# A hybrid decoder layer on one core: down products fetched two chunks at a time, one of them in 8 banks, seven products summed further in PSUM, tables fetched ahead

## The chip, the cores and the metric

The kernel runs on one core of a Trainium2 chip. The metric is device time in microseconds of one execution; the median of three runs of the kernel before is 2338.41 us (2338.2 to 2345.58). All arithmetic is on float32 data. TensorE multiplies in the type float32r; to keep the precision each operand is split into a rounded part ("hi") and the rest ("lo"), and a product is summed from three matmuls: hi by hi, hi by lo, lo by hi.

## The reference

One layer of a decoder for 1024 prompt tokens and 8 x 4 sample tokens: a half-step SwiGLU, a mixer (a state-space scan beside windowed attention), a cross-attention into 256 memory tokens, and a second half-step SwiGLU, each between two RMS norms. The change lies in the two SwiGLUs (and in the preparation of the scan's tables, which runs beside the first one). D_MODEL is 1024, D_FF 2816.

```python
def rms_norm(x, g):
    xf = x.astype(jnp.float32)
    y = xf * lax.rsqrt(jnp.mean(xf * xf, axis=-1, keepdims=True) + RMS_EPS)
    return (y * g.astype(jnp.float32)).astype(x.dtype)

def swiglu(x, w_gate, w_up, w_down):
    return (jax.nn.silu(x @ w_gate) * (x @ w_up)) @ w_down

def decoder_layer(x, ...):
    h = x
    h = h + 0.5 * rms_norm(swiglu(rms_norm(h, p['ffn1_pre_g']), ...), p['ffn1_post_g'])
    z = rms_norm(h, p['mix_pre_g']) @ p['w_in']
    ...
    h = h + rms_norm(mixed, p['mix_post_g'])
    c = memory_attend(rms_norm(h, p['xa_pre_g']), mem_k, mem_v, p['w_mem_q'], p['w_mem_o'])
    h = h + rms_norm(c, p['xa_post_g'])
    h = h + 0.5 * rms_norm(swiglu(rms_norm(h, p['ffn2_pre_g']), ...), p['ffn2_post_g'])
    return h, ...
```

## The kernel before

The 1056 tokens are three thirds ("t") of NT = 352, kept with the channels on the 128 partitions; `ORDER = (2, 0, 1)` gives ta = 2 (the one with the sample tokens), tb = 0, tc = 1. The hidden width 2816 is NH = 22 chunks of 128. A matmul has 128 weights columns and 352 tokens, and goes to one PSUM bank.

Order of the work in a SwiGLU:

1. Gate and up of the third ta: `gate_up` for each of the 22 chunks (48 matmuls each, line 106), the product goes to HBM scratch `h1[j][:, 2]`, one scratch tensor a chunk.
2. The down product of ta: `down` with parts `((0, 8),)`, that is, one pass in which all 8 banks (6 of the tag `mm`, 2 of the tag `px`) hold the 8 output blocks. In each chunk k it loads the hidden chunk (`raw2`, 352 wide; 2 buffers), splits it into `hid` (line 247 ACT for hi, 248 DVE for lo; `hid` holds two chunks and has 2 buffers), loads and splits the weights' chunk (`loadw`: `raw`, 2 buffers; line 100 ACT, 101 DVE into `w`, 6 buffers of 1024 columns), and runs 3 matmuls for each bank (line 252).
3. Gate and up of the thirds tb and tc together, the "pair stage": `pair_gate_up`. A 2 x 2 block product (two row blocks of 512 channels, two thirds) is done with seven products instead of eight (Strassen-Winograd). `pair_operands` makes the seven sums of the tokens once; `pair_weights` makes the seven sums of the weights for every two chunks (lines 307 ACT, 308 DVE, 312 to 318 DVE); `pair_products` runs the seven products (84 matmuls, line 327) and combines them into c11, c12, c21, c22 with copies (line 334 ACT) and adds out of PSUM (336, 342, 344, 346, 348 DVE). There are 22 such sets in a SwiGLU, 11 of the gate and 11 of the up weights.
4. The down products of tb and tc. In the first SwiGLU both go in two passes of 4 banks, `((0, 4), (4, 4))`, and each pass reads the whole hidden tensor anew; in the second SwiGLU the first of them goes in one pass of 8.

After each down product follow the post-norm with the residual (`post1` or `finish2`: squares on ACT, their sum on DVE line 117, a few small matmuls of lines 152 and 144 for the statistic, lines 220 and 221 on DVE) and, in the first SwiGLU, the next norm's halves (`pre1`). The statistics use the two `px` banks.

Beside the first SwiGLU the scan's tables are prepared: `ssm_prep` is a generator of 42 pieces (phase1, small_tables, 8 of `tables`, 32 of `groups`; two pieces of `groups` make a pair with two transposes, line 691, and four small matmuls, line 697, in the `px` banks). `step()` runs the next piece; the stages call it as a "filler" between their own pieces: 9 times in gate/up, not in the first down product, once at each of the 22 fillers of the pair stage, and once a chunk in the last down products until none is left. `tables(q)` loads its start values `t0` from scratch right before it uses them.

What sets the order: a scheduler takes the instructions of the whole program with the program's order as priority, simulates them, and writes one fixed order for each engine; engines then wait for each other through semaphores. An engine runs its instructions strictly in that order. Loads go through SyncE's queue (SP), stores through ACT's.

Of the kernel before, what the change touches and what calls it, by code (L numbers as in the profile page):

```python
# [14 lines left out]
NT = 352  # L15
# [13 lines left out]
def decoder_step(tc, a, o):  # L29
# [208 lines left out]
    def down(wd, h, y, parts, rs=None, filler=lambda: None):  # L238
        for c0, n in parts:
            p = [bank() if c < 6 else pbank() for c in range(n)]  # L240
            for k in range(NH):
                if k % 2 == 0:
                    pair = hidden(2)
                x = R("raw2", [128, 1024], 2)[:, :NT]
                hi, lo = pair[:, k % 2, 0], pair[:, k % 2, 1]
                sy.dma_start(x, h[k])
                sc.activation(hi, x, AF.Copy)  # L247
                v.tensor_sub(lo, x, hi.bitcast(F32))  # L248
                w = loadw(wd[k][:, c0 * 128:(c0 + n) * 128], width=n * 128)
                for c in range(n):  # L250
                    for q, (wa, xa) in enumerate(PASSES):
                        pe.matmul(p[c][:, :NT], w[:, wa, c * 128:c * 128 + 128], (hi, lo)[xa],  # L252
                                  start=k == 0 and q == 0, stop=k == NH - 1 and q == 2)
                filler()
            for c in range(n):
                if rs is not None:
                    v.tensor_mul(y[:, c0 + c], p[c][:, :NT], rs)  # L257
                elif c % 2:
                    v.tensor_copy(y[:, c0 + c], p[c][:, :NT])
                else:  # L260
                    sc.activation(y[:, c0 + c], p[c][:, :NT], AF.Copy)
# [33 lines left out]
    def pair_weights(src, j, raws):  # L295
# [4 lines left out]
        free, ops = [], {}  # L300
# [9 lines left out]
        halves_of("a11", a11)  # L310
        halves_of("a22", a22)
# [11 lines left out]
    def pair_products(w, x, first, c12, c21, c22):  # L323
        def product(p, a_, b_, start=False, stop=True):
            for k in range(4):
                for i, (wa, xa) in enumerate(PASSES):
                    pe.matmul(p, w[a_][:, wa, k * 128:k * 128 + 128], x[b_][xa][:, k],  # L327
                              start=start and k == 0 and i == 0, stop=stop and k == 3 and i == 2,
                              skip_group_check=True)
# [4 lines left out]
        sc.activation(u, pa, AF.Copy)
        product(pb, "s2", "t2", True, True)
        v.tensor_add(u, u, pb)
# [5 lines left out]
        v.tensor_add(z, u, pc)  # L342
        product(pd, "s1", "t1", start=True)
        v.tensor_add(c22, z, pd)
        product(pc, "a22", "t4", stop=True)
        v.tensor_add(c21, u, pc)
        product(pd, "s4", "b22", stop=True)
        v.tensor_add(c12, u, pd)

    def pair_gate_up(x, wg, wu, hs, home, filler=lambda: None):  # L350
        gs = K8(home).rearrange("p (i k) n -> p i k n", i=2)

# [5 lines left out]
        for j in range(NH // 2):  # L358
            g = gs[:, j % 2]
            h = hidden(2).bitcast(F32).rearrange("p a b n -> p (a b) n")  # L360
            pair_products(pair_weights(wg, j, raws(0)), x, lambda p: sc.activation(g[:, 0], p, AF.Silu),
                          g[:, 1], g[:, 2], g[:, 3])
            sc.activation(g[:, 1:4], g[:, 1:4], AF.Silu)
            filler()
            pair_products(pair_weights(wu, j, raws(1)), x, lambda p: v.tensor_mul(h[:, 0], g[:, 0], p),
                          h[:, 1], h[:, 2], h[:, 3])
            v.tensor_mul(h[:, 1:4], h[:, 1:4], g[:, 1:4])
            for i in range(2):
                sc.dma_start(hs[2 * j + i], h[:, 2 * i:2 * i + 2])
            filler()  # L370
# [94 lines left out]
    def ssm_prep():  # L465
# [28 lines left out]
        cre, cim = take(32), take(32)  # L494
        base = pos[0]
# [126 lines left out]
        def small_tables():  # L622
# [7 lines left out]
            for q in range(8):  # L630
                sc.dma_start(t16[q], T[:, :, 4 * q:4 * q + 4])

        def tables(q):
# [4 lines left out]
            sc.activation(T[:, :, :, 0:16], t0, AF.Copy)  # L638
# [751 lines left out]
    pair_gate_up(ops, a["wg2"], a["wu2"], [h[:, 0:2] for h in h2], 2)  # L1390
# [130 lines left out]
```

## Time and profile before

| | |
|---|---|
| median of 3 runs | 2338.41 us |
| the profiled execution | 2338.15 us, its span 2336.4 us |
| mean granted clock of TensorE | 0.987 |
| PE busy | 2241.9 us, 96% of the span |
| DVE busy | 1667.1 us, 71% |
| ACT busy | 991.9 us, 42% |
| moved by DMA | 359.26 MB, mean 154 GB/s |

Stages by their matmuls (us from the span's start): gate/up of ta to 183, its down product to 269, pair stage 273 to 582, down products of tb and tc 582 to 822, mixer and cross-attention to about 1563, second gate/up of its first third to 1750, its down product to 1836, second pair stage to 2130, the last two down products to 2318, and the last norm to 2336.

How to read it: engines are PE (TensorE's matmuls), PEld (its weight loads), DVE (VectorE), ACT (ScalarE), POOL and SP. The profiler's matmul records overlap, since matmuls are pipelined: their mean is about twice the step between their starts. So a stage is judged by the number of matmuls in it. A name such as `w<-raw` is the written and the read tile; L100 is line 100; "DMA raw<-wd" is a load into the tile raw from the tensor wd.

### The profile page before, as it was taken

How to read it: one execution, taken by the hardware profiler on the slowest of the kernel's cores; microseconds unless marked ns; L12 is line 12 of the kernel's file. 1: busy time of each engine (PE TensorE's matmuls, PEld its weight loads, DVE VectorE, ACT ScalarE, POOL GpSimd, SP SyncE). 2: the span in 40 equal slices, each digit the busy share in tenths (PEclk: the TensorE clock that was granted, in tenths of full speed). 3: DMA queues.
4: the chain of work that ended last, by engine and by line, in shares of the span. 5: the costliest groups of instructions: out<-in, count | busy, mean ns of one | idle time of the engine just before them, and what ended most of it. 6: DMA issues, size and time to landing. Idle time of an engine off the chain costs nothing.

```text
span 2336.4 us, 37554 instructions
## 1 busy us (share of the span) xinstructions
PE 2241.9 (96%) x14141; PEld 2133.5 (91%) x14141; DVE 1667.1 (71%) x3621; ACT 991.9 (42%) x1872; POOL 8.6 (0%) x22
## 2 busy tenths in 40 slices
PE   8999999999788999999899989999999999999997
PEld 8999999999777899788699869999999999999987
DVE  7987899778657566777768855488746787775465
ACT  6434334434445522435644323344335433433353
POOL 0000000000000000000000000000000000000000
PEclk9999999999999999999899999999999999999998
DMA  7566545333676621544135562256656343326564
GB/s 257 177 185 206 170 152 163 114 118 120 202 212 196 206 91 55 183 143 131 49 97 158 168 231 80 64 164 200 221 165 203 109 150 110 103 97 191 166 201 144
DMA packets 167477, 359.26 MB, mean 154 GB/s; under 512 B 20064, under 2 KB 90208, under 8 KB 165856
## 3 DMA queue, kind: packets, MB, share of 16 engines
q1 hardware_dynamic: 118720, 298.28, 40.8%
q10 hardware_dynamic: 48576, 58.59, 7.2%
q8 instruction: 111, 1.82, 0.3%
q14 instruction: 70, 0.57, 0.1%
HBM read 300.32 MB, written 59.59 MB: 154 GB/s over the span
## 4 chain that ended last, share of the span: by engine, by line
PE 53%; DMA 11%; DVE 6%; ACT 3%; issue 1%; ACTq 0%; SPq 0%; DVEq 0%
PE mm L106 17%; PE mm L327 13%; PE mm L252 6%; DMA raw<-wd 5%; PE px L106 3%; DVE w L101 2%; PE px L252 2%; DMA raw<-h 2%; ACT w L100 1%; PE cs L1253 1%; PE cv L1278 1%; PE ac L876 1%; PE px L457 1%; PE px L1175 1%; DVE K L220 1%
## 5 line engine op out<-in xcount | busy, mean ns | idle before, releaser
L106 PE MATMUL mm<-X,w 128*128 128x352 f32 x4272 | 709.3, 326 | 10.8 <-ACT X L196 7.1
L106 PEld LDWEIGHTS mm<-X,w 128*128 128x128 f32 x4272 | 685.8, 188 | 25.5 <-ACT X L196 7.3
L252 PE MATMUL mm<-hid,w 128*128 128x352 f32 x2772 | 486.7, 331 | 39.9 <-ACT hid L247 25.7
L101 DVE TENSOR_TENSOR w<-raw,w 128x1024 fp32r<-128x1024 f32 (+1 forms) x359 | 368.5, 1028 | 198.4 <-ACT w L100 197.2
L252 PEld LDWEIGHTS mm<-hid,w 128*128 128x128 f32 x2772 | 456.0, 191 | 58.4 <-ACT hid L247 36.9
L100 ACT ACTIVATE w<-raw 128x1024 fp32r<-128x1024 f32 (+1 forms) x359 | 322.4, 900 | 412.4 <-DMA raw<-wd 129.3
L327 PE MATMUL mm<-xq,w 128*128 128x352 f32 x2112 | 359.8, 324 | 4.0 <-DVE K L257 4.0
L327 PEld LDWEIGHTS mm<-xq,w 128*128 128x128 f32 x2112 | 342.4, 189 | 6.0 <-DVE K L257 4.3
L307 ACT ACTIVATE w<-raw 128x512 fp32r<-128x512 f32 x308 | 178.4, 624 | 206.2 <-PE mm L327 119.8
L308 DVE TENSOR_TENSOR w<-raw,w 128x512 fp32r<-128x512 f32 x308 | 202.2, 687 | 15.8 <-ACT w L307 11.8
L327 PE MATMUL mm<-X,w 128*128 128x352 f32 x1056 | 185.7, 324 | 1.2 <-DVE sq L342 0.7
L327 PEld LDWEIGHTS mm<-X,w 128*128 128x128 f32 x1056 | 171.0, 188 | 3.3 <-DVE sq L342 1.0
L248 DVE TENSOR_TENSOR hid<-raw,hid 128x352 fp32r<-128x352 f32 x198 | 97.9, 521 | 64.5 <-ACT hid L247 60.1
L247 ACT ACTIVATE hid<-raw 128x352 fp32r<-128x352 f32 x198 | 90.6, 490 | 98.4 <-DMA raw<-h 50.9
L476 DVE TENSOR_TENSOR K<-K 128x256 f32<-128x256 f32 (+4 forms) x380 | 106.9, 320 | 26.2 <-DMA sp<-K 9.2
L117 DVE TENSOR_TENSOR tot<-tot,sq 128x352 f32<-128x352 f32 x179 | 93.1, 521 | 9.7 <-ACT sq L115 6.5
L327 PE MATMUL mm<-K,w 128*128 128x352 f32 x528 | 99.7, 326 | 0.0
L115 ACT ACTIVATE sq<-K 128x352 f32<-128x352 f32 x170 | 81.1, 488 | 35.7 <-DVE tot L117 26.1
L327 PEld LDWEIGHTS mm<-K,w 128*128 128x128 f32 x528 | 88.3, 190 | 0.3 <-ACT w L307 0.3
L252 PE MATMUL px<-hid,w 128*128 128x352 f32 x396 | 75.4, 324 | 0.0
L252 PEld LDWEIGHTS px<-hid,w 128*128 128x128 f32 x396 | 66.2, 188 | 0.0
L1210 ACT ACTIVATE K<-mm 128x352 f32<-128x352 f32 x48 | 22.3, 464 | 89.4 <-PE mm L106 89.2
(328 smaller groups left out, 2186.9 us busy)
## 6 DMA issues: line engine op xcount, KB each, us to landing
raw<-wu SPq DMA_DIRECT2D x87, 512.0 KB
raw<-wg SPq DMA_DIRECT2D x86, 512.0 KB
raw<-h SPq DMA_DIRECT2D x198, 176.0 KB
raw<-wd SPq DMA_DIRECT2D x66, 512.0 KB
raw<-wd SPq DMA_DIRECT2D x132, 256.0 KB
h<-hid ACTq DMA_DIRECT2D x44, 352.0 KB
sp<-sp SPq DMA_DIRECT2D x16, 848.0 KB
h<-K ACTq DMA_DIRECT2D x9, 1408.0 KB
```

The source lines that it names most:

```text
L100: sc.activation(w[:, 0], raw, AF.Copy)
L101: v.tensor_sub(w[:, 1], raw, w[:, 0].bitcast(F32))
L106: pe.matmul(p, w[:, wa, col:col + 128], x[xa][:, k, :n], start=first and i == 0, stop=last and i == 2)
L115: sc.activation(q, c, AF.Square)
L117: eng.tensor_add(tot, tot, q)
L247: sc.activation(hi, x, AF.Copy)
L248: v.tensor_sub(lo, x, hi.bitcast(F32))
L252: pe.matmul(p[c][:, :NT], w[:, wa, c * 128:c * 128 + 128], (hi, lo)[xa], start=k == 0 and q == 0, stop=k == NH - 1 and q == 2)
L307: sc.activation(w[:, 0], x, AF.Copy)
L308: v.tensor_sub(w[:, 1], x, w[:, 0].bitcast(F32))
L327: pe.matmul(p, w[a_][:, wa, k * 128:k * 128 + 128], x[b_][xa][:, k], start=start and k == 0 and i == 0, stop=stop and k == 3 and i == 2, s ...
L476: v.tensor_tensor(out, x, y, op)
```

## The change

Four things are changed.

- `down` takes the chunks two at a time: one load and one split for two hidden chunks (the scratch is now one tensor of 22 chunks for each third), and in a pass of 4 banks two loads of 512 columns into the two halves of one `raw` buffer with one split of 1024 columns. In a pass of 8 banks the weights are loaded as before. The down product of tb in the first SwiGLU goes in one pass of 8 banks instead of two of 4.
- `pair_products` sums further in PSUM: the bank pa takes P1, then s2t2, s3t3 and a22t4 on top, read in between (p1, u, z) or at the end; pd takes s1t1 and s4b22. Two adds on DVE are left out; two ACT copies come in. The last two products of a set run after the first product of the next set, and the sets share half-used weight tiles (`free`).
- The preparation's steps lie elsewhere: 4 in gate/up, 7 in the first down product (in chunks 0, 2, ..., 12), then two at each filler of the pair stage, but for the 12th, which holds `post1` of ta and the sum of squares of its next norm; `pre1_late` is left with the halves.
- `t0` is loaded one table ahead, into space of the tables that is free by then.

```diff
     def down(wd, h, y, parts, rs=None, filler=lambda: None):
         for c0, n in parts:
             p = [bank() if c < 6 else pbank() for c in range(n)]
-            for k in range(NH):
-                if k % 2 == 0:
-                    pair = hidden(2)
-                x = R("raw2", [128, 1024], 2)[:, :NT]
-                hi, lo = pair[:, k % 2, 0], pair[:, k % 2, 1]
-                sy.dma_start(x, h[k])
-                sc.activation(hi, x, AF.Copy)
-                v.tensor_sub(lo, x, hi.bitcast(F32))
-                w = loadw(wd[k][:, c0 * 128:(c0 + n) * 128], width=n * 128)
-                for c in range(n):
-                    for q, (wa, xa) in enumerate(PASSES):
-                        pe.matmul(p[c][:, :NT], w[:, wa, c * 128:c * 128 + 128], (hi, lo)[xa],
-                                  start=k == 0 and q == 0, stop=k == NH - 1 and q == 2)
-                filler()
+            for k in range(0, NH, 2):
+                x = R("raw2", [128, 1024], 2)[:, :2 * NT].rearrange("p (k n) -> p k n", k=2)
+                hid = hidden(2)
+                sy.dma_start(x, h[:, k:k + 2])
+                split(x, hid[:, :, 0], hid[:, :, 1])
+                if n == 8:
+                    ws = [loadw(wd[k + j]) for j in range(2)]
+                else:
+                    raw = wp.tile([128, 1024], F32, name="raw", tag="raw", bufs=2)
+                    for j in range(2):
+                        sy.dma_start(raw[:, 512 * j:512 * j + 512], wd[k + j][:, c0 * 128:c0 * 128 + 512])
+                    w = loadw(None, raw)
+                    ws = [w[:, :, 0:512], w[:, :, 512:1024]]
+                for j in range(2):
+                    for c in range(n):
+                        for q, (wa, xa) in enumerate(PASSES):
+                            pe.matmul(p[c][:, :NT], ws[j][:, wa, c * 128:c * 128 + 128], hid[:, j, xa],
+                                      start=k + j == 0 and q == 0, stop=k + j == NH - 1 and q == 2)
+                    filler()
...
-    def pair_products(w, x, first, c12, c21, c22):
+    def pair_products(w, x, out, c21):
...
-        pa, pb = bank()[:, :NT], bank()[:, :NT]
-        u = Q()
-        product(pa, "a11", "b11", start=True)
+        pa, pb, pd = (bank()[:, :NT] for _ in range(3))
+        p1, u, z = R("sg", [128, NT], 2), Q(), Q()
+        product(pa, "a11", "b11", True)
+        sc.activation(p1, pa, AF.Copy)
+        yield
+        product(pb, "a12", "b21", True)
+        v.tensor_add(out[:, 0], p1, pb)
+        product(pa, "s2", "t2", False)
         sc.activation(u, pa, AF.Copy)
-        product(pb, "s2", "t2", True, True)
-        v.tensor_add(u, u, pb)
-        product(pa, "a12", "b21", stop=True)
-        first(pa)
-        pc, pd = bank()[:, :NT], bank()[:, :NT]
-        z = S()
-        product(pc, "s3", "t3", start=True)
-        v.tensor_add(z, u, pc)
-        product(pd, "s1", "t1", start=True)
-        v.tensor_add(c22, z, pd)
-        product(pc, "a22", "t4", stop=True)
-        v.tensor_add(c21, u, pc)
-        product(pd, "s4", "b22", stop=True)
-        v.tensor_add(c12, u, pd)
+        product(pd, "s1", "t1", True)
+        product(pa, "s3", "t3", False)
+        sc.activation(z, pa, AF.Copy)
+        v.tensor_add(out[:, 2], z, pd)
+        yield
+        product(pa, "a22", "t4", False)
+        c21(pa)
+        product(pd, "s4", "b22", False)
+        v.tensor_add(out[:, 1], u, pd)
+        yield
...
+        def finish(n, steps, h):
+            next(steps)
+            j, g = n // 2, gs[:, n // 2 % 2]
+            if n % 2 == 0:
+                sc.activation(g[:, 0:3], g[:, 0:3], AF.Silu)
+            else:
+                v.tensor_mul(h[:, 0:3], h[:, 0:3], g[:, 0:3])
+                for i in range(2):
+                    sc.dma_start(hs[i][:, 2 * j:2 * j + 2], h[:, 1:3] if i else h[:, 0::3])
             filler()
...
+        for n in range(NH):
...
+            steps = pair_products(pair_weights(src, j, raws(n), free), x, out, c21)
+            next(steps)
+            if prev:
+                finish(*prev)
+            next(steps)
+            prev = n, steps, h
+        finish(*prev)
...
-            tmp, t0 = take(512), take(128).rearrange("p (z g c) -> p z g c", z=2, c=16)
-            sy.dma_start(t0, t16[q])
-            sc.activation(T[:, :, :, 0:16], t0, AF.Copy)
+            tmp = take(512)
+            if q < 7:
+                sy.dma_start(t0[(q + 1) % 2], t16[q + 1])
+            sc.activation(T[:, :, :, 0:16], t0[q % 2], AF.Copy)
...
-    h1 = [scratch(f"h1_{j}", [128, 3, NT]) for j in range(NH)]
+    h1 = [scratch(f"h1_{t}", [128, NH, NT]) for t in range(3)]
...
-        if 5 <= j and j % 2:
+        if j in (5, 9, 13, 17):
             step()
...
-    down(a["wd1"], [h[:, 2] for h in h1], y, ((0, 8),), xa[2], lambda: step(F_A[1]))
+    down_steps = iter([1, 0] * 7)
+    down(a["wd1"], h1[2], y, ((0, 8),), xa[2], lambda: step(next(down_steps, 0)))
     ops = pair_operands(xr[tb], xr[tc_], tc_, ta)
-    post1(ta, y)
-    pair_gate_up(ops, a["wg1"], a["wu1"], [h[:, 0:2] for h in h1], tb, lambda: step(F_A[2]))
+    seen, late = [], []
+
+    def between():
+        seen.append(1)
+        if len(seen) == 12:
+            post1(ta, y)
+            late.append(pre_rstd(y))
+        elif len(seen) > 0:
+            step(2)
+
+    pair_gate_up(ops, a["wg1"], a["wu1"], h1[:2], tb, between)
     xp[0].release()
     xp[0] = pool("x1b", "left")
-    pre1(ta, y)
+    pre1_late(ta, y, late[0])
     for i, t in enumerate((tb, tc_)):
         y = K8((tc_, tb)[i])
-        down(a["wd1"], [h[:, i] for h in h1], y, ((0, 4), (4, 4)), filler=lambda: step(F_A[3]))
+        down(a["wd1"], h1[i], y, (((0, 8),), ((0, 4), (4, 4)))[i], filler=lambda: step(F_A[3]))
```

More of the change, by code (lines that the diff above doesn't have):

```diff
@@ L293, in pair_operands, with pair_weights @@
         return ops
-    def pair_weights(src, j, raws):
+    def pair_weights(src, j, raws, free):
         r1, r2 = raws
@@ L299, in pair_weights @@
         a11, a12, a21, a22 = r1[:, 0:512], r1[:, 512:1024], r2[:, 0:512], r2[:, 512:1024]
-        free, ops = [], {}
+        ops = {}
         def halves_of(name, x):
@@ L310, in pair_weights @@
         halves_of("a11", a11)
+        halves_of("a12", a12)
         halves_of("a22", a22)
@@ L315, in pair_weights, with product @@
         halves_of("s2", a11)
-        halves_of("a12", a12)
+        halves_of("s1", a22)
         halves_of("s3", a21)
         v.tensor_sub(a12, a12, a11)
-        halves_of("s1", a22)
         halves_of("s4", a12)
         return ops
-    def pair_products(w, x, first, c12, c21, c22):
-        def product(p, a_, b_, start=False, stop=True):
+    def pair_products(w, x, out, c21):
+        def product(p, a_, b_, start):
             for k in range(4):
@@ L356, in raws @@
             return [wp.tile([128, 1024], F32, name="raw", tag="raw", bufs=2) for _ in range(2)]
[L358 to L363, printed above, removed]
-            filler()
[L365 to L370, printed above, removed]
+        def finish(n, steps, h):
[7 more added lines that the diff above has]
+                    sc.dma_start(hs[i][:, 2 * j:2 * j + 2], h[:, 1:3] if i else h[:, 0::3])
+            filler()
+        for n in range(NH):
+            j, g = n // 2, gs[:, n // 2 % 2]
+            if n % 2 == 0:
+                h, out, src = None, g, wg
+                c21 = lambda p, g=g: sc.activation(g[:, 3], p, AF.Silu)
+            else:
+                h = hidden(2).bitcast(F32).rearrange("p a b n -> p (a b) n")
+                out, src = h, wu
+                c21 = lambda p, g=g, h=h: v.tensor_mul(h[:, 3], g[:, 3], p)
+            steps = pair_products(pair_weights(src, j, raws(n), free), x, out, c21)
[5 more added lines that the diff above has]
+        finish(*prev)
     def norm_in_place(y, gi):
@@ L494, in ssm_prep @@
         cre, cim = take(32), take(32)
+        t0 = [t[:, 0:128].rearrange("p (z g c) -> p z g c", z=2, c=16) for t in (tbc, tbs)]
         base = pos[0]
@@ L727, in pre1, with pre1_late @@
         mid[t] = prenorm(t, y, G_MIX_PRE)
+    def pre1_late(t, y, rs):
+        mid[t] = halves(t, y, G_MIX_PRE) + (rs,)
     ta, tb, tc_ = ORDER
-    h1 = [scratch(f"h1_{j}", [128, 3, NT]) for j in range(NH)]
+    h1 = [scratch(f"h1_{t}", [128, NH, NT]) for t in range(3)]
     w = wp.tile([128, 2, 1024], F32R, name="w", tag="w", bufs=6)
@@ L1379, in finish2 @@
             sc.dma_start(o["yT"][t, :, k:k + 2], y[:, k:k + 2])
-    h2 = [scratch(f"h2_{j}", [128, 3, NT]) for j in range(NH)]
+    h2 = [scratch(f"h2_{t}", [128, NH, NT]) for t in range(3)]
     for j in range(NH):
-        gate_up(xn[0], (loadw(a["wg2"][j]), loadw(a["wu2"][j])), h2[j][:, 2])
+        gate_up(xn[0], (loadw(a["wg2"][j]), loadw(a["wu2"][j])), h2[2][:, j])
     y = K8(3)
-    down(a["wd2"], [h[:, 2] for h in h2], y, ((0, 8),), xn[0][2])
+    down(a["wd2"], h2[2], y, ((0, 8),), xn[0][2])
     finish2(0, y)
@@ L1389, in decoder_step @@
     ops = pair_operands(xn[1], xn[2], 1, 0)
-    pair_gate_up(ops, a["wg2"], a["wu2"], [h[:, 0:2] for h in h2], 2)
+    pair_gate_up(ops, a["wg2"], a["wu2"], h2[:2], 2)
     for i, parts in ((0, ((0, 8),)), (1, ((0, 4), (4, 4)))):
         y = K8((3, 2)[i])
-        down(a["wd2"], [h[:, i] for h in h2], y, parts)
+        down(a["wd2"], h2[i], y, parts)
         finish2(1 + i, y, i)
```

7 lines of the change are left out of this document (4 added, 3 removed).

## The prediction

> **What bounds the kernel now.** First the page: which engine is full, and where it is not. The second and third rows are tenths of busy time in 40 slices of 58 us.
>
> ```profile
> PE 2241.9 (96%) x14141; PEld 2133.5 (91%) x14141; DVE 1667.1 (71%) x3621; ACT 991.9 (42%) x1872; POOL 8.6 (0%) x22
> PE   8999999999788999999899989999999999999997
> PEld 8999999999777899788699869999999999999987
> ```
>
> TensorE is the bound nearly everywhere; it thins out in slices 11 to 14 (582 to 822 us), in the attention and memory stages, which the change leaves alone, and near the end. A busy PE is no proof of full speed, so the second view counts matmuls: the windows of busy time, first of line L252 (the down products) alone, then of all engines. After the stretch and its length come PE busy and its count, PEld, (DVE, ACT, POOL), the granted clock, the DMA share and GB/s.
>
> ```profile
> 582.00:640.00 58.00, 35.84 (x177) 32.59 (x177) 0.91 0.63 198
> 640.00:700.00 60.00, 52.90 (x304) 48.46 (x304) 1.00 0.71 213
> 700.00:738.00 38.00, 32.79 (x195) 31.09 (x193) 1.00 0.62 193
> 738.00:760.00 22.00, 14.39 (x65) 13.12 (x66) 0.84 0.63 207
> 2145.00:2223.00 78.00, 78.00 (x483) 78.00 (x482) 1.00 0.56 169
> 2223.00:2318.00 95.00, 87.59 (x514) 82.29 (x512) 1.00 0.64 194
> ...
> 269.00:273.00 4.00, 0.23 (x1) 0.24 (x2) 3.86 (x12) 0.98 (x3) 0.00 (x0) 0.76 0.75 230
> 273.00:582.00 309.00, 307.77 (x1897) 300.78 (x1898) 262.16 (x540) 127.63 (x248) 0.00 (x0) 0.99 0.40 130
> 582.00:822.00 240.00, 204.43 (x1161) 188.73 (x1160) 147.75 (x316) 120.75 (x248) 1.95 (x2) 0.96 0.66 203
> 1836.00:2130.00 294.00, 294.00 (x1840) 294.00 (x1840) 227.34 (x400) 118.31 (x200) 0.00 (x0) 1.00 0.35 113
> 2130.00:2145.00 15.00, 13.89 (x86) 13.56 (x86) 8.37 (x10) 5.02 (x6) 0.00 (x0) 1.00 0.81 265
> 2223.00:2318.00 95.00, 89.57 (x542) 85.41 (x541) 57.20 (x112) 46.15 (x89) 0.00 (x0) 1.00 0.64 194
> ```
>
> The row 2145 to 2223 is the ruler: a down product in one pass of 8 banks, 78.00/483 = 161.5 ns a matmul, no idle time. A chunk of the hidden width is 24 matmuls there, 3.88 us, and 12 in a pass of 4 banks, 1.94 us. The second FFN's pair stage (294 us) is at that floor too. The 4-bank passes are not: 640 to 700 should hold 60/0.1615 = 371 matmuls and holds 304. Next, who is waited for in 582 to 822 (busy sum, mean ns, then idle time before and its causes):
>
> ```profile
> L252 PE MATMUL mm<-hid,w 128*128 128x352 f32 x1056 | 192.0, 339 | 33.3 <-ACT hid L247 21.9 <-DVE hid L248 10.5 <-ACT K L261 0.7
> L697 PE MATMUL px<-K 128*16 128x128 f32 x24 | 3.7, 275 | 0.6 <-ACT rs L158 0.6
> L144 PE MATMUL px<-c_ident,ti 118*128 118x118 f32 x18 | 2.7, 285 | 1.7 <-DVE ti L134 1.7
> L691 PE MATMUL px<-c_ident,K 128*128 128x128 f32 x12 | 2.4, 280 | 0.0
> L152 PE MATMUL px<-ones,tot 128*118 128x1 f32 x18 | 2.0, 230 | 0.0
> L100 ACT ACTIVATE w<-raw 128x512 fp32r<-128x512 f32 (+1 forms) x88 | 56.3, 644 | 63.1 <-DMA raw<-wd 56.2 <-DMA raw<-w_in 5.5 <-PE mm L252 0.5
> L247 ACT ACTIVATE hid<-raw 128x352 fp32r<-128x352 f32 x86 | 39.6, 491 | 27.1 <-DMA raw<-h 17.9 <-PE mm L252 3.9 <-DMA sp<-kd 3.4
> ```
>
> PE waits for the split of the hidden chunk, and ACT, in its order, for the weights' loads (56.2 us) and the hidden's (17.9). The chain of work shows the period:
>
> ```profile
> 658.72 0.64 ACT w L100
> ...
> 660.10 3.07 DMA raw<-wd
> 663.86 0.70 DVE w L101
> 664.58 3.02 DMA raw<-wd
> ```
>
> 660.10 to 664.58 is 4.48 us: load 3.07, ACT 0.64, DVE 0.70, hand-overs 0.07. Two raw buffers of one chunk each go round in that time, so a chunk takes 2.24 us and not 1.94: a ring bound by latency, since the DMA share there is 0.71, and 0.81 at 265 GB/s occurs elsewhere.
>
> **The change, part by part.** The profiled execution took 2338.15 us, a span of 2336.4 and 1.75 around it; the median of the runs is 2338.41, so a difference carries over as it is.
>
> *Down products (first FFN, 582 to 822).* The floor of this stretch: 1056 matmuls by 0.1615 = 170.5; 33 of the neighbours (1161 less 1056 less 72 small ones) 5.3; the small ones by their rows 3.7 + 2.7 + 2.4 + 2.0 = 10.8. Together 186.6; lost 53.4 of 240.
>
> The new ring: a raw buffer now holds two chunks of 512 columns from two loads, and is split once at 1024 wide. Rows for that width, and for the wait at 269, which comes next:
>
> ```profile
> L101 DVE TENSOR_TENSOR w<-raw,w 128x1024 fp32r<-128x1024 f32 x45 | 55.0, 1224 | 11.2 <-ACT w L100 11.1
> L100 ACT ACTIVATE w<-raw 128x1024 fp32r<-128x1024 f32 x45 | 47.6, 1059 | 65.8 <-DMA raw<-wu 26.7 <-DMA raw<-wg 20.4 <-DVE K L476 9.2
> 268.73 3.55 DVE L476 TENSOR_TENSOR K<-K 128x128 f32<-128x128 f32 x10 [1.72 <-ACT K L638]
> 272.77 1.54 PE L327 MATMUL mm<-xq,w 128*128 128x352 f32 x4 [3.98 <-DVE K L257]
> ```
>
> Two loads into one buffer were not seen. At best they land together, 3.07; at worst the second adds its transfer, 256 KB at the 265 GB/s of row 2130, 1.0, and an issue of 0.3: 4.4. I take 4.2, near the worst. With 1.06 + 1.22 + 0.1 a round is 6.6 us for four chunks, 1.65 a chunk, under 1.94: PE becomes the bound. The queue must carry 432 KB in 1.94 us, 228 GB/s; share 0.66 at 203 GB/s scales to 0.74. The hidden's pair is one load and one split: by slope between 352 and 1024 wide ACT takes about 0.79 and DVE 0.89 for two chunks where two singles took 0.98 and 1.04. All of that lies beside PE: 2.1 us of DVE in 3.88.
>
> The first of the two products (microbatch 0) becomes one pass of 8 banks: no second read of h, 22 splits fewer, and the ruler's row says it costs no wait. It takes both px banks for 85 us, which the norms and the prep's transposes use too; the prep is over by then and the late norm has its rstd already, so nothing queues for them.
>
> What stays lost: entering the stage 2 (row 2130 to 2145 loses 15 - 86 x 0.1615 = 1.1, and the late halves of ta come on top); the norm between the two products 5 (738 to 760 lost 22 - 65 x 0.1615 = 11.5 with one chunk a buffer; twice the chunks in raw and hidden loads ride out about half; ends 2 and 11.5); the 4-bank passes 2; the last norm 2. Sum 11, ends 5 and 25. The stretch gains 53.4 - 11 = 42.4, and 6.1 more (L697, L691) leaves it with the prep.
>
> *Prep steps moved.* Before, 9 steps ran in gate/up, 22 in the pair stage, the last 11 here. After: 4 in gate/up, 7 in the first down product, then two at each of the pair stage's fillers. PE's 6.1 us come back there. On DVE the pair stage loses two adds of 22 sets (PSUM sums instead) and gains five prep pairs and the first part of ta's second norm:
>
> ```profile
> L476 DVE TENSOR_TENSOR K<-K 128x288 f32<-128x288 f32 (+4 forms) x117 | 39.7, 368 | 7.2 <-DMA sp<-K 5.0 <-PE px L691 0.9 <-PE px L697 0.9
> L336 DVE TENSOR_TENSOR q<-q,mm 128x352 f32<-128x352 f32 x22 | 11.4, 517 | 0.4 <-PE mm L327 0.4
> L117 DVE TENSOR_TENSOR tot<-tot,sq 128x352 f32<-128x352 f32 x8 | 4.2, 521 | 0.0
> L220 DVE SCALAR_TENSOR_TENSOR K<-K,c_gains,y 128x352 f32<-128x352 f32 x8 | 4.1, 584 | 0.0
> L327 PE MATMUL mm<-xq,w 128*128 128x352 f32 x1044 | 180.9, 326 | 4.0 <-DVE K L257 4.0
> L327 PE MATMUL mm<-X,w 128*128 128x352 f32 x516 | 91.4, 325 | 1.2 <-DVE sq L342 0.7 <-ACT q L334 0.6
> ```
>
> Less 2 x 22 x 0.517 = 22.7; plus 5 x 39.7/11 = 18; plus about 6 (L117 again, and small ones): 262 stays about 263, in 315 us. I take 2 us of new waits; ends -2 and 15 (rival 2). Net of this part: +8.1.
>
> *First down product, end.* At 268.73 ten table operations sat on DVE ahead of the bank's evacuation, and PE waited 3.98. The tables now run between chunks 0 and 13 with their input loaded one table earlier, and DVE is free at the end: one evacuation and hand-over, 0.8, is left. Gain 3.2. On those 14 chunks DVE gets about 4 of 7.8 us per two chunks more, under its capacity with the 3.3 for splits; six w tiles cover a lag.
>
> *Seven products in PSUM.* Same 84 matmuls a set. Two copies of pa per set (after s2, after s3) must end while one other product, 1.94 us, runs. Before, one ACT copy and two adds stood in the same place, and in 22 sets PE waited 1.2 us for them (last row above; the 4.0 in the row ahead of it is the wait at 269). I take zero in both FFNs; the price if it fails is rival 3.
>
> *Second FFN.* Its last product in two passes of 4 (2223 to 2318): 95 - 514 x 0.1615 = 12.0, less 2.0 of small matmuls (89.57 - 87.59), 10.0 lost. Left: norm 2, ring 2. Gain 6.
>
> Sum: -42.4 - 6.1 + 8.1 - 3.2 - 6 = -49.6 against 2338.15: 2288.5.
>
> [...] In 582 to 640 and 738 to 760 the granted clock is 0.91 and 0.84, worth 58 x 0.09 + 22 x 0.16 = 8.7 of the lost 53.4; I count it as lost to the gaps, since it is 1.00 in 640 to 738, where the waits are shorter. The longest wait there is this row's, 3.0:
>
> ```profile
> PE mm L252 <- DVE hid L248: 10.5, 5, 3.0
> ```
>
> [...] The trace puts the low clock where the gaps are, so I keep 2288.5.
>
> **The rivals.**
> 1. *The 4-bank passes stay slow*, because the queue and not the ring sets 2.24. For: 213 GB/s is the most that stretch reached. Against: 265 at share 0.81. Price: 44 chunks by 0.30 = 13, and 6 not gained in the second FFN, less 4 counted: 15, so 2303.
> 2. *DVE becomes the bound of the first pair stage.* For: set 12 carries ta's post-norm and the next sum of squares, about 20 us, on top of 8 of its own in 13.6. Against: such a post-norm stood at that stage's start at 262/309 busy, and PE lost little. Price: the overrun, 15, less 2 counted: 2302.
> 3. *The other side: reading pa between products stalls PE.* If ACT reaches the copies late, each overrun d is paid twice a set in 44 sets, 88 x d. From d = 0.65 us (57 us) the change is slower than before by over 0.3%; at 0.75 it ends at 2354. Against: the 0.6 us that PE waited for L334. [...]
> 4. *The reads of two chunks come late.* h is one tensor of 22 chunks now; if a load waited for the last store and not for its own, four entries to a down product would each cost a store and a load, 3.07 each, and a split, about 7: 28, so 2316. Against: nothing in the code asks for it.
>
> **How the numbers follow.** Forecast 0.63, rival 1 0.12, rival 2 0.13, rival 3 0.04, rival 4 0.04, rest (the order of the later stages shifts, nothing gained) 0.04. Its own range is 2274 (entry, norms and rings at their lower ends) to 2298. For 8 in 10 I add rivals 1 and 2 and some drift of the stages behind: 2270 to 2308. 0.3% is 7 us, about what a measurement of this kernel can tell from no change. Faster 0.92: the forecast and rivals 1, 2 and 4; same 0.03 and slower 0.01 + 0.04: the rest and rival 3.
>
> **What would show it.** The stretch from the pair stage's last matmul to the projections shrinks from 240 to about 192; L100's wait for raw<-wd nearly goes; 4-bank passes step 1.94 a chunk; no wait of 4 us on L257's bank; the pair stage grows by some 8 us; PE's waits for the copies of pa stay under 3 us. Wrong would be: raw<-wd still ending ACT's waits in the 4-bank passes, gaps in the pair stage around its 12th set, or PE waiting there for ACT.

## The result and the profile after

The changed kernel takes 2319.11 us (median of 4 runs, 2316.77 to 2323.28), beside 2340.8 (4 runs, 2338.2 to 2345.58) for the kernel before on the same chip: a ratio of 0.9907, interval 0.9883 to 0.9931. That is 22 us faster; 2288.5 was predicted, with 2308 as the upper end. The profiled execution took 2323.28 us, a span of 2321.5, and so lies 4 us above its median.

The page of the kernel after, the rows that answer to those of before (PE's busy time and the granted clock in tenths, 40 slices of 58 us):

```profile
PE   8999999999999999999899999995999999999997
...
PEclk9999999999999999999899999997999999999998
```

The slices 11 to 13, thin before, are full. Slice 28 (1567 to 1625 us), which was full before, has fallen to 5, and its clock to 7.

The same stages in windows, cut at the start of the same matmul in each kernel: to the pair stage of the first FFN; the pair stage; the two down products and the first projections; mixer and memory stage up to the first norm matmul of the memory stage's output projection; from there (the rest of that projection, its norms, gate/up of the second FFN) to the second FFN's first down product; the rest. After the stretch and its length stand PE, PEld, DVE, ACT and POOL busy, the clock, the DMA share and GB/s. Before:

```profile
0.00:272.77 272.77, 260.79 (x1601) 258.15 (x1601) 219.99 (x539) 119.88 (x170) 0.20 (x4) 1.00 0.67 207
272.77:587.91 315.14, 313.91 (x1934) 306.92 (x1934) 267.48 (x551) 131.98 (x257) 0.00 (x0) 0.99 0.40 130
587.91:900.83 312.92, 276.27 (x1610) 259.38 (x1610) 186.77 (x408) 133.59 (x269) 1.95 (x2) 0.97 0.55 171
900.83:1515.80 614.97, 592.11 (x4038) 520.67 (x4036) 431.30 (x1191) 263.52 (x625) 6.46 (x16) 0.98 0.39 127
1515.80:1750.33 234.53, 232.31 (x1455) 226.90 (x1454) 166.26 (x272) 97.86 (x147) 0.00 (x0) 1.00 0.58 185
1750.33:2336.36 586.03, 566.51 (x3512) 561.48 (x3510) 395.29 (x663) 245.03 (x406) 0.00 (x0) 0.99 0.46 148
```

After:

```profile
0.00:275.04 275.04, 263.88 (x1600) 260.48 (x1601) 220.28 (x529) 119.29 (x159) 0.20 (x4) 0.99 0.68 205
275.04:596.45 321.41, 320.08 (x1991) 310.61 (x1992) 262.93 (x561) 154.85 (x323) 0.00 (x0) 1.00 0.49 150
596.45:855.25 258.80, 252.71 (x1554) 250.22 (x1553) 152.34 (x254) 102.35 (x147) 1.95 (x2) 0.99 0.52 165
855.25:1476.29 621.04, 597.04 (x4038) 524.80 (x4036) 431.28 (x1191) 263.92 (x625) 7.52 (x16) 0.97 0.39 126
1476.29:1738.42 262.13, 235.62 (x1454) 229.38 (x1454) 169.03 (x270) 97.83 (x145) 0.00 (x0) 0.95 0.54 167
1738.42:2321.47 583.05, 563.92 (x3512) 562.22 (x3510) 370.77 (x555) 248.81 (x386) 0.00 (x0) 0.99 0.48 148
```

| stage | before | after | difference | forecast |
|---|---|---|---|---|
| to the first pair stage | 272.77 | 275.04 | +2.3 | -3.2 |
| first pair stage | 315.14 | 321.41 | +6.3 | +8.1 |
| two down products, first projections | 312.92 | 258.80 | -54.1 | -48.5 |
| mixer and memory stage | 614.97 | 621.04 | +6.1 | 0 |
| last norms, gate/up of the second FFN | 234.53 | 262.13 | **+27.6** | 0 |
| second FFN from its first down product | 586.03 | 583.05 | -3.0 | -6 |
| sum | | | -14.9 | -49.6 |

The first FFN as a whole did what was forecast (-45.6 against -43.6), in part by luck: two misses of opposite sign cancel, 5.5 us too little up to the pair stage and 5.6 too much behind it. The loss sits at the entry to the second FFN, whose gate/up code the change doesn't alter but for the tensor it stores to. There the chain of `norm_in_place` for the last third ends in one matmul of ones on the summed squares (`rstd_wide`, L164). The timeline of PE after:

```profile
1576.63 0.75 PE L164 MATMUL px<-tot,ones 128*128 128x352 f32 x2
1576.95 1.55 PE L106 MATMUL mm<-X,w 128*128 128x352 f32 x7
1599.97 1.54 PE L164 MATMUL px<-tot,ones 128*128 128x352 f32 x2 [21.47 <-DVE tot L117]
1605.41 6.78 PE L106 MATMUL mm<-X,w 128*128 128x352 f32 x26 [3.90 <-DVE sg L233]
```

and of before:

```profile
1618.52 0.75 PE L164 MATMUL px<-tot,ones 128*128 128x352 f32 x2
1618.84 34.03 PE L106 MATMUL mm<-X,w 128*128 128x352 f32 x210
1653.95 0.86 PE L164 MATMUL px<-tot,ones 128*128 128x352 f32 x2 [1.08 <-DVE tot L117]
```

The last norm's matmul (the second L164 of each) stood 210 gate/up matmuls behind the one before it; now it stands 7 behind. PE runs in its fixed order, so it waits 21.47 us for a chain of DVE, while hundreds of gate/up matmuls stand queued behind the norm. The chain, from DVE's timeline after:

```profile
1584.12 4.06 DVE L220 SCALAR_TENSOR_TENSOR K<-K,c_gains,y 128x352 f32<-128x352 f32 x8
...
1597.93 0.53 DVE L221 TENSOR_TENSOR K<-K,K 128x352 f32<-128x352 f32 x1 [0.65 <-DMA K<-h]
...
1599.39 0.53 DVE L117 TENSOR_TENSOR tot<-tot,sq 128x352 f32<-128x352 f32 x1 [0.50 <-ACT sq L115]
```

It is the post-norm's own work and its residual loads; before, it ran under 34 us of gate/up. What has gone is the cover. The second wait, 3.90, has the same source: ACT issues the store of the first two gate/up chunks at 1598.89, behind the squares of that norm, and the two `sg` buffers come free late. Idle time is not the whole of the 27.6: the same matmuls keep PE busy for 235.62 us against 232.31, at a clock of 0.95 against 1.00 over the stage, so some 3.3 us of it are the lower clock behind the wait.

### The profile page after: what moved, and what is told of

Its sections match the earlier page's. It is cut to its first block, busy times and chain, and to the rows that moved or that the text cites. A ratio compares the mean times of both kernels' runs of the same rounds, so it can differ in the third digit from the quotient of the medians.

```text
span 2321.5 us, 36671 instructions
## 1 busy us (share of the span) xinstructions
PE 2233.3 (96%) x14141; PEld 2137.7 (92%) x14141; DVE 1606.6 (69%) x3357; ACT 987.1 (43%) x1784; POOL 9.7 (0%) x22
## 4 chain that ended last, share of the span: by engine, by line
PE 81%; DVE 8%; DMA 7%; ACT 2%; issue 1%; ACTq 1%; SPq 0%; DVEq 0%
PE mm L106 26%; PE mm L333 21%; PE mm L257 14%; PE px L106 3%; PE px L257 3%; DMA sp<-K 1%; PE cs L1290 1%; DVE K L497 1%; PE cv L1315 1%; DVE w L101 1%; PE px L1212 1%; PE ac L913 1%; DVE K L220 1%; PE px L478 1%; DVE K L221 1%
## 5 line engine op out<-in xcount | busy, mean ns | idle before, releaser
L100 ACT ACTIVATE w<-raw 128x1024 fp32r<-128x1024 f32 x293 | 309.1, 1056 | 387.9 <-PE mm L106 112.6
L101 DVE TENSOR_TENSOR w<-raw,w 128x1024 fp32r<-128x1024 f32 x293 | 358.3, 1223 | 163.8 <-ACT w L100 161.1
L257 PE MATMUL mm<-hid,w 128*128 128x352 f32 x2640 | 455.2, 327 | 13.8 <-DVE hid L185 7.5
L257 PEld LDWEIGHTS mm<-hid,w 128*128 128x128 f32 x2640 | 432.6, 189 | 18.2 <-DVE hid L185 10.3
L333 PE MATMUL mm<-xq,w 128*128 128x352 f32 x2112 | 364.5, 323 | 1.9 <-DVE K L262 1.3
L185 DVE TENSOR_TENSOR hid<-raw,hid 128x704 fp32r<-128x704 f32 x88 | 78.2, 890 | 92.3 <-ACT hid L184 87.2
L184 ACT ACTIVATE hid<-raw 128x704 fp32r<-128x704 f32 x88 | 69.5, 789 | 142.9 <-PE px L257 59.2
L257 PE MATMUL px<-hid,w 128*128 128x352 f32 x528 | 101.9, 327 | 0.0
L257 PEld LDWEIGHTS px<-hid,w 128*128 128x128 f32 x528 | 89.6, 190 | 0.0
```

The costliest lines, as they stand in the source:

```text
L100: sc.activation(w[:, 0], raw, AF.Copy)
L101: v.tensor_sub(w[:, 1], raw, w[:, 0].bitcast(F32))
L257: pe.matmul(p[c][:, :NT], ws[j][:, wa, c * 128:c * 128 + 128], hid[:, j, xa], start=k + j == 0 and q == 0, stop=k + j == NH - 1 and q == 2)
```

## The experiments

Eleven more kernels were measured. Each ratio is to the kernel before on the same chip (2335.65, 2337.34 and 2337.49 us on the three that were used) and is worked out from the means of the runs, not from their medians; differences in us go by the ratios where no two times stand beside them.

In the diffs `down_o` and `pair_gate_up_o` are the functions of the kernel before, but for the tensors that they store to.

**Is it the order?** The first suspects for what moved it were the scratch tensors, as the scheduler simulates the whole program: the change made the second FFN's hidden tensors three of 22 chunks instead of 22 of three. Run *reuse_h1*, one line:

```diff
-    h2 = [scratch(f"h2_{t}", [128, NH, NT]) for t in range(3)]
+    h2 = h1
```

> The changed kernel with one line altered: the second FFN's hidden activations go into the first FFN's three scratch tensors instead of three new ones. Nothing computed differs. Theory (order): the changed kernel lost 27.6 us at the entry to the second FFN because the fixed order puts the last third's norm matmul 7 gate/up matmuls behind the norm before it, where it had 210; with the reused tensors it stands 209 behind again, PE finds work, and 2319.1 becomes about 2292 (2288 to 2296). Rival 1 (supply): the residual and weight loads are late there whatever the order is, PE waits at another matmul, and the time stays at 2319 (2315 to 2323). Rival 2 (half): the chain of the norm takes 20 us of DVE and ACT work that then delays the gate/up products, about 2305.

Measured 2286.69 us (2284.97 to 2287.18), ratio 0.9787 (0.9774 to 0.9801), a little under the range of its theory. Timeline of PE at that place, and its windows:

```profile
1572.26 0.76 PE L164 MATMUL px<-tot,ones 128*128 128x352 f32 x2
1572.58 33.87 PE L106 MATMUL mm<-X,w 128*128 128x352 f32 x209
1606.29 0.76 PE L164 MATMUL px<-tot,ones 128*128 128x352 f32 x2
```

```profile
595.42:854.19 258.77, 252.58 (x1554) 250.09 (x1553) 152.13 (x254) 102.21 (x147) 1.95 (x2) 0.99 0.52 165
854.19:1468.89 614.70, 591.71 (x4038) 520.81 (x4036) 431.06 (x1191) 263.56 (x625) 7.51 (x16) 0.98 0.39 127
1468.89:1702.12 233.23, 232.09 (x1456) 226.95 (x1454) 166.09 (x270) 97.75 (x145) 0.00 (x0) 1.00 0.59 187
```

The norm is 209 matmuls behind again, the stage takes 233.23 us and the whole gap is gone; the rivals of supply and of half the gain both fall. The mixer stage, whose code no kernel here alters, takes 614.70 us here, 621.04 in the trace of after, 614.97 before, and 614.2 to 620.4 in the others; of the 6.3 between the first two, 5.3 are PE's own busy time, at a clock of 0.98 against 0.97. So the +6.1 of the table can't be put down to the change. (Up to the first pair stage, too, the kernels with the change's code there scatter by some 3 us, 274.2 to 277.6.)

**The inverse.** *before_whole_h2* puts only the three whole tensors into the kernel before (and so makes two stores of one in the second pair stage, which comes later than the norm):

```diff
-    h2 = [scratch(f"h2_{j}", [128, 3, NT]) for j in range(NH)]
+    h2 = [scratch(f"h2_{t}", [128, NH, NT]) for t in range(3)]
...
-        gate_up(xn[0], (loadw(a["wg2"][j]), loadw(a["wu2"][j])), h2[j][:, 2])
+        gate_up(xn[0], (loadw(a["wg2"][j]), loadw(a["wu2"][j])), h2[2][:, j])
```

> The kernel before with one thing of the change: the second FFN's hidden activations go into three tensors of 22 chunks instead of 22 tensors of three chunks; all products, passes and loads stay as they were, and the first FFN is untouched. Theory (order): the tensors alone change the fixed order at the entry to the second FFN (norm matmul 7 behind the one before it, not 210), so the gap appears here too: 2340.8 + 27 = 2368 (2362 to 2373). Rival 2b (shift): the gap comes from the first FFN's shorter stretch, which lets the middle run against late loads; then 2341 (2337 to 2345). Rival 1 (supply) also gives 2341.

Measured 2361.62 us, ratio 1.0104 (1.0089 to 1.0120): 24 us slower, with no matmul, pass or load changed, and just under the range of its theory.

```profile
1618.14 1.55 PE L106 MATMUL mm<-X,w 128*128 128x352 f32 x7
1640.41 1.54 PE L164 MATMUL px<-tot,ones 128*128 128x352 f32 x2 [20.72 <-DVE tot L117]
```

The same 7 and nearly the same wait, so neither the first FFN nor the products have a part in it.

**Tensor or order?** *before_third_whole* gives the kernel before one whole tensor for the third that gate/up writes:

```diff
-    h2 = [scratch(f"h2_{j}", [128, 3, NT]) for j in range(NH)]
+    h2 = [scratch(f"h2_{j}", [128, 2, NT]) for j in range(NH)]
+    h2a = scratch("h2_a", [128, NH, NT])
...
```

> The kernel before with one new tensor of 22 chunks for the hidden activations that the second FFN's gate/up writes chunk by chunk, and 22 tensors of two chunks for the others. The fixed order keeps the norm matmul 208 gate/up matmuls behind the one before it. Theory (order): no gap, the time of before, 2336 (2332 to 2341). Rival (tensor): storing chunk by chunk into one tensor, or reading it back, is what costs the time, with any order: 2362 as with three whole tensors.

Measured 2338.27 us, ratio 1.0006 (0.9997 to 1.0015), with the norm 208 matmuls behind:

```profile
1618.85 33.75 PE L106 MATMUL mm<-X,w 128*128 128x352 f32 x208
1652.44 0.79 PE L164 MATMUL px<-tot,ones 128*128 128x352 f32 x2
```

Storing chunk by chunk into one new tensor costs nothing by itself; the placement does. What in the tensors makes the scheduler place the norm early was not found: three new whole tensors do, reused ones and this mixture don't.

**The whole second FFN as before**, *ffn2_old* (22 tensors of three chunks, one chunk at a time, old pair stage there; first FFN as changed):

```diff
-    h2 = [scratch(f"h2_{t}", [128, NH, NT]) for t in range(3)]
+    h2 = [scratch(f"h2_{j}", [128, 3, NT]) for j in range(NH)]
...
-    pair_gate_up(ops, a["wg2"], a["wu2"], h2[:2], 2)
+    pair_gate_up_o(ops, a["wg2"], a["wu2"], [h[:, 0:2] for h in h2], 2)
...
-        down(a["wd2"], h2[i], y, parts)
+        down_o(a["wd2"], [h[:, i] for h in h2], y, parts)
```

> The changed kernel with its whole second FFN put back to the form before (22 tensors of three chunks, one chunk at a time, old pair stage); the first FFN as changed. Theory: the order at the entry to the second FFN is that of before, so nothing is lost there, and the second FFN's own change was worth 3 us (583.1 against 586.0 from the first down matmul to the end): 2287 + 3 = 2290 (2287 to 2294). Rival: the first FFN's change and not the second FFN's tensors moved the norm; then 2319 + 3 = 2322.

Measured 2293.56 us, ratio 0.9814 (0.9799 to 0.9829): 6.3 us (0.0027) above *reuse_h1*. Its second FFN takes 584.9 us from the first down product to the end, that of *reuse_h1* 581.05. So the change's second FFN, with its tensors, cost about 27 and gave 4 to 6.

**The parts of the first FFN**, each undone on *reuse_h1*. *one_chunk_down*, the ring of the two later products:

```diff
-        down(a["wd1"], h1[i], y, (((0, 8),), ((0, 4), (4, 4)))[i], filler=lambda: step(F_A[3]))
+        down_o(a["wd1"], [h1[i][:, k] for k in range(NH)], y, ((0, 4), (4, 4)), filler=lambda: step(F_A[3]))
```

> The kernel of the first run (reused tensors), with the two down products behind the first pair stage put back to one chunk at a time in two passes of 4 banks each; the first down product, the prep's place and the pair stage stay as changed. Theory: the ring is worth the 42 us of the prediction's sum, so about 2292 + 42 = 2334 (2328 to 2340), and ACT waits for raw<-wd again. Rival (prep): most of the gain of that stretch came from the prep having left it, and the ring alone gives 20 or less: 2312 or below.

Measured 2319.43 us, ratio 0.9932 (0.9919 to 0.9945): 34 us (0.0145) worse than *reuse_h1*, between the two expectations; in the traces 28.0 of it lie in the stretch behind the pair stage (286.79 against 258.77).

*old_prep* puts back the prep's steps, ta's post-norm and its second norm where they were:

```diff
-        if j in (5, 9, 13, 17):
+        if 5 <= j and j % 2:
...
-    down(a["wd1"], h1[2], y, ((0, 8),), xa[2], lambda: step(next(down_steps, 0)))
+    down(a["wd1"], h1[2], y, ((0, 8),), xa[2], lambda: step(F_A[1]))
...
-    pair_gate_up(ops, a["wg1"], a["wu1"], h1[:2], tb, between)
+    post1(ta, y)
+    pair_gate_up(ops, a["wg1"], a["wu1"], h1[:2], tb, lambda: step(F_A[2]))
...
-    pre1_late(ta, y, late[0])
+    pre1(ta, y)
```

> The kernel of the first run (reused tensors) with the prep's steps, ta's post-norm and its second norm put back where they stood before the change (9 steps in gate/up, none in the first down product, one at each filler of the pair stage, the rest in the two down products behind it). Theory (prep): the one-chunk kernel still gained 26 us between the pair stage's last matmul and the first transpose of the attention part, with the old ring; that came from the prep having left. So with the prep back the stretch loses about 26 and the stages ahead of it give back some 14 (pair stage 321 to 310, first down product 3): about 2299 (2294 to 2304). Rival (ring): the prep costs only the 6.1 us of PE that the prediction counted there and the new ring hides the rest; then 2286.7 + 6 - 14 = 2279 (2275 to 2283).

Measured 2306.26 us, ratio 0.9871 (0.9853 to 0.9888), 19.6 us worse, more than either expectation. The stretch behind the pair stage (same cuts as above), *one_chunk_down* and then *old_prep*:

```profile
598.36:885.15 286.79, 262.90 (x1555) 250.04 (x1554) 172.00 (x350) 126.93 (x244) 1.95 (x2) 0.98 0.54 168
```

```profile
594.66:867.41 272.75, 261.55 (x1590) 255.82 (x1589) 165.07 (x301) 108.98 (x171) 1.95 (x2) 0.97 0.56 175
```

From 312.92, the ring with the prep where it was gives -40.2, the prep's leaving with the old ring -26.1, both -54.1. They overlap by 12, and no run shows by itself why. *old_prep*'s pair stage is only 2.4 us shorter than that of *reuse_h1* (318.9 against 321.3), not 11. The stretch and the pair stage make 11.6 of its 19.6 us; 5.7 lie in the mixer stage, where equal code scatters as much. So the prep's new place is worth 11.6 to 19.6.

*old_pair* has the old `pair_weights`, `pair_products` and `pair_gate_up` in both FFNs:

```diff
-    pair_gate_up(ops, a["wg1"], a["wu1"], h1[:2], tb, between)
+    pair_gate_up_o(ops, a["wg1"], a["wu1"], h1[:2], tb, between)
...
-    pair_gate_up(ops, a["wg2"], a["wu2"], h2[:2], 2)
+    pair_gate_up_o(ops, a["wg2"], a["wu2"], h2[:2], 2)
```

> The kernel of the first run (reused tensors), with both pair stages put back to the old form: sums of products on DVE, four banks, no overlap of one set with the next. Theory of the prediction: seven products summed in PSUM are worth zero, 2292 (2289 to 2295). Rival (as the changed kernel's second pair stage suggests, 295.2 against 293.5 us between its first and last matmul): PE waits for the copies out of the shared bank, 1.7 us a stage and somewhat more in the first, so the old form gives 2286 to 2289. Other side: with the prep's adds on DVE the old form no longer fits beside PE in the first stage, 2300.

Measured 2302.56 us, ratio 0.9859 (0.9843 to 0.9875): 17 us worse; the side that was not believed in. Its first pair stage, and the largest of PE's waits there (the sum, times, the longest):

```profile
277.52:615.00 337.48, 324.91 (x1979) 314.27 (x1980) 284.47 (x606) 139.31 (x281) 0.00 (x0) 0.98 0.46 143
```

```profile
PE px L152 <- DVE tot L117: 3.2, 1, 3.2
```

337.5 us against 321.3, with DVE busy for 284 instead of 262, and PE idle for 12.6 us instead of 0.9, most of it waiting for DVE, at a clock of 0.98 instead of 1.00. The moved prep and the old form don't both fit beside PE. The old form has 44 adds more on DVE, but it also lacks the overlap of one set with the next, and no run separates the two.

*old_pair_second* has the old form in the second FFN alone (the second edit above):

> The kernel of the first run (reused tensors) with the old pair stage in the second FFN alone. The prediction gave the PSUM sums zero there; the stage has 302.0 us with the new form and 299.5 with the old one (from its first to the following product's matmuls, with a few matmuls of neighbours more in the new one). Theory (beside PE): nothing but these neighbours differs, 2286.7, 2285 to 2288. Rival (copies): PE does wait for the copies out of the shared bank, and the old form is 2 to 3 us faster: 2284. As the DVE is at 70% in that stage in the new form and 77% in the old, a gain like the first stage's 16 us is not expected: 2303 would mean that DVE is the bound there too.

Measured 2287.94 us, ratio 0.9786 (0.9771 to 0.9801): no difference. So in the second FFN, where no prep runs beside it, the old form costs nothing.

*two_passes* undoes the single pass of the second product:

```diff
-        down(a["wd1"], h1[i], y, (((0, 8),), ((0, 4), (4, 4)))[i], filler=lambda: step(F_A[3]))
+        down(a["wd1"], h1[i], y, ((0, 4), (4, 4)), filler=lambda: step(F_A[3]))
```

> The kernel of the first run (reused tensors) with the down product of the first of the two later microbatches put back to two passes of 4 banks, but in the new ring of two chunks. Theory of the prediction: a 4-bank pass in the new ring runs at PE's pace, so the second read of h and 22 more splits are hidden: 2287 (2284 to 2291). Rival (one pass): a good part of the ring's 33 us came from the pass of 8 banks, which loads a weight chunk for twice the products; then 2293 to 2303, with waits for raw<-wd.

Measured 2291.91 us (2287.81 to 2294.98), ratio 0.9803 (0.9786 to 0.9819), between the two expectations, with an interval that overlaps that of *reuse_h1*. In its place, from the pair stage to the attention, it takes 259.1 us against 258.8: the pass count is worth nothing that these runs can tell.

**An attempt at more.** *spread_first* takes ta's eight halves from ahead of the down product and calls one at each chunk; *spread_both* does the same with the next third's post-norm and halves:

```diff
-    pre1_late(ta, y, late[0])
+    work = late_halves(ta, y, late[0])
...
-        down(a["wd1"], h1[i], y, (((0, 8),), ((0, 4), (4, 4)))[i], filler=lambda: step(F_A[3]))
+        down(a["wd1"], h1[i], y, (((0, 8),), ((0, 4), (4, 4)))[i], filler=lambda: next(work, None))
```

> The kernel of the first run (reused tensors); ta's eight pairs of halves (one ScalarE and one VectorE instruction each) no longer stand together ahead of the down product behind the first pair stage but one at each chunk of it. In the changed kernel seven of them run on DVE from 599.2 to 602.8, PE waits 2.06 and 0.93 us around 601 and 605, and the granted clock is 0.50 for about 6.8 us behind that. Theory (gap and clock): with the gap gone the clock stays at 1.00 there, and 3.0 + 3.4 us come back: 2286.7 - 6 = 2281 (2278 to 2284). Rival (clock by itself): the dip of the clock comes with the stage and not with the gap, 3 us come back: 2284. Rival (ring): the chunks behind are as late, since the first loads set the entry: 2287.

> The kernel of the run before this one, and in the last down product of the first FFN the post-norm and the halves of the microbatch before it are also spread, one step at each chunk, where they stood together ahead of it. Theory: PE's short waits of 0.6 to 0.85 us between 700 and 740 (3 us in all) go: another 2 to 3 us, 2279 (2275 to 2283). Rival (late): the projections then wait for that norm, which ends 19 chunks into the last product, or the attention part's order changes: 2285 to 2295.

Measured 2284.78 us, ratio 0.9785 (0.9766 to 0.9803), and 2288.77 us, ratio 0.9799 (0.9786 to 0.9813): no gain. The theories were not put to the test, since the gap did not go. PE in *spread_first*:

```profile
604.89 1.27 PE L257 MATMUL mm<-hid,w 128*128 128x352 f32 x6 [2.14 <-ACT hid L184]
```

Moving the calls did not move the work: the scheduler still placed all eight halves on DVE between 599 and 606 us, and DVE's split of `hid` behind them. The short waits that *spread_both* aimed at stayed too: of the 40 us from 700 on, PE is busy for 37.02, in *spread_first* for 36.97. As the gap stayed, these runs decide nothing about the clock. *reuse_h1*, one line away from the change, beats both kernels.

## Why the prediction was wrong

*The step that failed* is the sum's silence on stages that the change doesn't touch. Later stages were carried over as they were, with 0.04 for "the order of the later stages shifts, nothing gained". The new scratch tensors were looked at once, in rival 4, and only for loads that wait for stores; they moved one matmul in PE's order, from 210 gate/up matmuls behind the norm before it to 7, and the stage took 27.6 us longer. Rival 4's 2316 lies near the result by accident: its price was four entries to down products that are late by about 7 us, and PE's longest wait for a split of `hid` is 2.7. With the order mended the same sum holds: 2286.69 measured beside 2335.65, a difference of 49.0, against the forecast of 49.6. That it fits so well is in part luck; its parts fit less well:

- *Down products, -42.4, and 6.1 for the prep.* Together -54.1. The ring with the single pass gives -40.2 with the prep where it was, as forecast; the prep costs 14.0 on top of the new ring (*old_prep* against *reuse_h1*), and not its PE time of 6.1 alone. Of the 14.0, 6.0 are its matmuls, some 3 a lower clock (0.97 against 0.99), and 5.0 new idle time of PE, which waits longer for the splits of `hid` (9.4 against 6.1) and once for `rs` of ACT (1.8); the step counted the first alone. What stays lost, forecast 11: 6.1 of PE idle (258.80 less 252.71; half of it at the entry) and some 3 of lower clock (0.94 in 582 to 640). ACT's rows of the stretch after:

```profile
L100 ACT ACTIVATE w<-raw 128x1024 fp32r<-128x1024 f32 x45 | 47.4, 1052 | 38.0 <-DMA raw<-wd 20.5 <-PE px L257 15.1 <-PE mm L257 2.5
L184 ACT ACTIVATE hid<-raw 128x704 fp32r<-128x704 f32 x32 | 25.3, 790 | 47.9 <-PE mm L257 22.1 <-PE px L257 20.5 <-DMA raw<-h 5.1
```

  ACT's wait for `raw<-wd` fell from 56.2 to 20.5 us, and the split of the hidden now waits for PE to free its buffers: PE is the bound, as step one said. Rival 1 did not come: the 4-bank passes lose 3.0 us in four short waits beside the norm (of 0.59 to 0.85, up to 725), and in 737 to 760 PE has no idle time and runs 146 matmuls, about the ruler's pace. The two-chunk split takes 0.79, as estimated.
- *Pair stage, +8.1.* Measured +6.3, DVE 262.9 us busy for the 263 forecast. The forecast held with the new form: with the old one, and so without the 22.7 us that it set against the moved work, the stage overran by 16 (*old_pair*), which is rival 2's mechanism and nearly its price.
- *End of the first down product, -3.2.* The wait on the bank fell from 3.98 to 1.34, but the stage grew by 3.0 (93.14 against 90.13). "DVE is free at the end" was wrong: six operations of the prep stand ahead of the last split of `hid`, for which PE now waits 2.06, and six more ahead of the evacuation. The clock is lower, too: 0.83 in 265 to 275, before 0.89 in 265 to 272.8. DVE, and PE, after:

```profile
260.81 2.62 DVE L497 TENSOR_TENSOR K<-K 128x128 f32<-128x128 f32 x6
263.35 0.89 DVE L185 TENSOR_TENSOR hid<-raw,hid 128x704 fp32r<-128x704 f32 x1
...
271.94 2.61 DVE L497 TENSOR_TENSOR K<-K 128x256 f32<-128x256 f32 x6
274.46 0.52 DVE L262 TENSOR_TENSOR K<-mm,rs 128x352 f32<-128x352 f32 x1
```

```profile
264.29 4.18 PE L257 MATMUL mm<-hid,w 128*128 128x352 f32 x17 [2.06 <-DVE hid L185]
...
275.04 1.24 PE L333 MATMUL mm<-xq,w 128*128 128x352 f32 x6 [1.34 <-DVE K L262]
```

- *Seven products in PSUM, 0.* Right: 0.9786 with and 0.9787 without the old form in the second FFN, and rival 3's waits for the copies come to 0.5 us there.
- *Second FFN, -6.* From its first down product on, -3.0 in the trace of after and -5.0 in *reuse_h1*; the runs put 6.3 on it, with the pair stage's form and the tensors. Right, within the noise.
- *Tables loaded ahead.* No run undoes this part of the change by itself; what it is worth stays open.
- *The clock, 8.7 us taken as the gaps' own.* Half right. In 738 to 760 it went from 0.84 to 1.00, as the gaps went (22 x 0.16 = 3.5 us). At the entry it still falls, to 0.50, with two short waits left (2.06 and 0.93); the rows of the last section show it.

## What to carry to other kernels

When the order of the instructions comes out of a simulated schedule, any edit can change the order of the whole program: ahead of costing a change, list what it alters that the scheduler sees (tensors, buffers, tags), and give the untouched stages a range of their own. Ahead of blaming an engine for a gap, count the independent instructions that stand between two waits on the stalled engine, before and after: 210 against 7 told the cause, and one line repaired it. A work item moved beside PE is costed on the engine that it shares with the critical splits, and whether it fits depends on what else in the change frees that engine.

## What was not expected of the hardware

Single waits of PE of a little over 2 us were followed by half the granted clock, 0.50. After, around a wait of 2.06 us, and before, around one of 2.22 us; each time PE's row, then the windows:

```profile
602.88 1.50 PE L257 MATMUL mm<-hid,w 128*128 128x352 f32 x6 [2.06 <-ACT hid L184]
600.00:604.00 4.00, 1.94 (x12) 1.65 (x11) 4.00 (x8) 3.27 (x4) 0.00 (x0) 0.96 0.64 214
604.00:608.00 4.00, 3.07 (x11) 2.61 (x10) 2.65 (x3) 0.00 (x0) 0.00 (x0) 0.50 0.89 281
608.00:612.00 4.00, 4.00 (x20) 4.00 (x19) 0.00 (x0) 0.96 (x1) 0.00 (x0) 0.69 1.02 395
```

```profile
611.22 6.98 PE L252 MATMUL mm<-hid,w 128*128 128x352 f32 x32 [2.22 <-ACT hid L247]
608.00:612.00 4.00, 1.78 (x13) 1.29 (x12) 0.95 (x2) 1.75 (x5) 0.00 (x0) 1.00 0.70 204
612.00:616.00 4.00, 4.00 (x17) 4.00 (x17) 3.72 (x9) 2.06 (x7) 0.00 (x0) 0.57 0.58 171
```

By windows of 1 us (after 0.83 in 603 to 604 and 0.75 in 610 to 611, before 0.72 in 612 to 613 and 0.58 in 615 to 616, 0.50 between) the clock fell about a microsecond behind the gap and stayed at 0.50 for some 7 us after and 3 us before. By the rows that is at most 4 x (0.04 + 0.50 + 0.31) = 3.4 us and 4 x 0.43 = 1.7 us of full speed, on top of the wait itself. Not every such wait was followed by a fall. After, the longer one at the entry to the second FFN's later down products left the clock at 1.00:

```profile
2133.97 1.24 PE L257 MATMUL mm<-hid,w 128*128 128x352 f32 x6 [2.73 <-ACT hid L184]
2134.00:2138.00 4.00, 4.00 (x24) 3.88 (x25) 3.32 (x4) 1.76 (x2) 0.00 (x0) 1.00 0.64 212
2138.00:2142.00 4.00, 4.00 (x27) 4.00 (x26) 1.23 (x1) 1.06 (x1) 0.00 (x0) 1.00 0.85 264
```

The clock fell behind waits of 2.06 and 2.22 us and not behind one of 2.73. So here the length of a wait alone does not tell whether the clock falls, and no run settles what does.
